# A first modulation by halves of the features, and inverse roots as one power operation on GpSimd

## The chip, the core and the metric

The kernel runs on one core of one Trainium2 chip. The core has five engines: TensorE (PE; its weight loads are listed apart as PEld), VectorE (DVE), ScalarE (ACT), GpSimd (POOL) and SyncE (SP), which here issues most DMAs. Each engine works off its own queue of instructions in order; semaphores tie the queues together. The metric is the device time of one execution in microseconds, the median of several.

## What is computed

Two layers of a backbone over 640 tokens: 512 latent tokens and a prompt of 128, with 1024 features each. The prompt has conditioning of its own, so that scale and shift come in two variants, one for the latent tokens and one for the prompt. Cut to what matters here:

```python
def trunk_layer(x, cond, grid, ctx, ...):
    sh1, sc1, gt1, sh2, sc2, gt2 = modulation(cond, w_mod, b_mod)   # silu(cond) @ w_mod + b_mod
    h = rms_norm(x, g_norm_mix) * (1.0 + sc1) + sh1
    rq, rk, rv, rg, qn, qr, ckv, kr = project(h, w_in, ...)         # h @ w_in; qa, kva, kr normed per row
    ...                                                             # retention, latent attention
    x = x + gt1 * (jnp.concatenate([ret, attn], axis=-1) @ w_o)
    h = rms_norm(x, g_norm_ffn) * (1.0 + sc2) + sh2
    gate, up = jnp.split(h @ w_ffn_in, 2, axis=-1)
    x = x + gt2 * ((jax.nn.silu(gate) * up) @ w_ffn_out)

def rms_norm(x, g):
    y = x * lax.rsqrt(jnp.mean(x * x, axis=-1, keepdims=True) + EPS)
    return y * g
```

Inverse square roots stand in three places: the norms over 1024 features (one root per token), the norms of the low-rank parts qa, kva and kr (three roots per token), and the norms of keys and queries per head.

## The kernel before

The 640 tokens are five tiles of 128, the fifth the prompt; tokens lie on partitions for norms, and features lie on partitions for the operands of a projection. The 1024 features are eight k steps of 128. A float32 product is made of three products of rounded parts: each operand is split into a high part, a rounded copy, and a low part, the rest, and `mm3` (L373 to L375) multiplies high by high, high by low and low by high. So every operand costs a copy (ACT as a rule) and a subtraction (DVE).

A planner puts each engine's instructions in order by the order of the program and by when their operands are ready. `tc.keep_in_program_order` (called `pin`) ties an instruction behind the one that the program put before it on the same engine. Buffers come from pools: 20 large ones of 128 x 1280 (`big`: X0, the operand T, and `wm`, the pieces of modulation weights, share them), 20 of 128 x 512 (`slot`), 12 for weights of 128 x 1024 (`wgt`), and small ones. `prefetch(n)` issues loads of the next weights on SP's queue and splits them into high and low parts (L356, L357) until weights of cost n are ready; `take` hands them out.

The **front** of the first layer (L653 to L668) runs so. `first_norm` (L577) takes for each tile two sums of squares on ACT, one inverse root, the scaling of x (L534), the transposes on PE (L537), and copies into X0, features on partitions. `first_half(i, dst)` (L245) loads 1024 of the modulation's columns, eight pieces of 512 KB on SP's queue, multiplies them by the conditioning on PE (L261, 16 products), adds the bias on DVE (`rows`, L265) and transposes the result into `modT`. It is called for all scale columns first, then for all shift columns. Behind the scales come `gain` (G1 = gain of the norm times one plus scale) and `first_scale` (L584), which multiplies X0 by G1, half on DVE, half on ACT. Then come `prefetch(6)` and `load_consts`, and behind the shifts `first_shift` (L595), which makes the high part on ACT (L603) and the low part in one fused DVE operation, tokens in the groups of `FIRST_MOD`: the first tile, two tiles, two tiles. Then `weave` mixes the projection `low_first` (`low_steps`, L684: eight k steps of 416 columns a tile into `low`, squares on ACT, three roots a token, `lown` at L695 and L696, transposes at L718, `ck` and `qa` behind them), the next modulations (`gemv_steps`, L219, of which `gemv1` loads into the large buffers that X0 and the halves leave), and others.

The **inverse roots**: `rsqrt_of` (L377) does a guess by bits and three Newton steps on DVE, eight operations for one column (L381 to L387) and eleven for three. `rsqrt_act` (L395) takes a logarithm and an exponential on ACT and one Newton step of three operations on DVE. `rsqrt_of` is called 20 times for one column: by `inv_rms` (L522) in `first_norm`, in `norm_quarters` (L557) at the entry of the FFN in both layers, and in `norm_steps` at the start of the second layer, where the roots of all five tiles come first; and ten times for three columns in `low_steps`. `rsqrt_act` is called twice in each of four `pair_steps` (L1013) a layer, for 12 columns of keys and 20 of queries; its result scales the keys, and the queries at L1075 and L1077, and `head_steps` transposes the queries on PE (L1098).

At the **layer boundary** the last projection of the first layer ends in `apply_gate` (`x`, L1230); POOL's queue issues the stores of x to DRAM (L1414); the norms of the second layer follow (`norm_mod`: x at L534, transposes at L537, `htmp`, and the high and low parts, L555). At the entry of the FFN `norm_quarters` writes quarters, and `operand` makes the high and low parts Mh and Ml (L1268).

## Time and profile before

| | |
|---|---|
| median of 3 runs | 1709.63 us (1708.22 to 1710.19) |
| the profiled execution | 1709.34 us |
| its span, first to last instruction | 1707.6 us |
| mean granted clock of TensorE | 0.989 |
| PE, DVE, ACT, POOL busy | 97%, 70%, 43%, 3% |

A row of the profile gives an engine, a line of the kernel, the operation, what it writes and reads by the program's names, the shape and a count. The span runs from the first to the last instruction; the execution's own time is 1.7 us longer. The granted clock is 1.00 where TensorE runs at 2.4 GHz and 0.50 at 1.2 GHz; a value between is a mean over a stretch with both.

### The profile page before, as it was taken

To read this page: it belongs to the slowest core of one execution; us is meant where nothing else is said; L and a number is where in the kernel's file an instruction comes from. 1 tells how busy PE (TensorE), PEld (TensorE's weight loads), DVE (VectorE), ACT (ScalarE), POOL (GpSimd) and SP (SyncE) were. 2 spreads that over 40 slices of the span, in tenths; PEclk is the share of its full clock that TensorE was granted. 3 is DMA by queue.
4 is the path that set the end of the run, shared out by engine and by line. 5 is a ranking of instruction groups with operands and counts; after the bars stand their busy time and mean duration, and the time that the engine had idled before them with its cause. 6 is when DMAs were issued, how large, how long until landed. Compare 5 with 4: busy or idle time off the path is not lost.

```text
span 1707.6 us, 26357 instructions
## 1 busy us (share of the span) xinstructions
PE 1651.3 (97%) x10166; PEld 1422.2 (83%) x10166; DVE 1194.9 (70%) x2670; ACT 741.2 (43%) x1598; POOL 56.4 (3%) x74
## 2 busy tenths in 40 slices
PE   6999999999999999999979999999999999999998
PEld 2789887667988898989959888776789899999987
DVE  5846569737966687776786455787388777686766
ACT  4532258734524242524344222687355243343422
POOL 0001210000000000000010021100000000000000
PEclk9999999999999999999989999999999999999999
DMA  9862101141226322313383420011312231212222
GB/s 325 306 224 70 35 17 32 38 133 65 74 76 218 134 91 76 106 50 112 113 321 105 144 64 26 19 29 62 125 63 90 71 112 62 99 50 99 75 74 87
DMA packets 65407, 173.77 MB, mean 102 GB/s; under 512 B 10353, under 2 KB 19953, under 8 KB 65281
## 3 DMA queue, kind: packets, MB, share of 16 engines
q1 hardware_dynamic: 64288, 169.20, 29.3%
q0 software_dynamic: 800, 2.62, 0.4%
q8 instruction: 80, 1.31, 0.3%
q14 instruction: 47, 0.38, 0.1%
q10 hardware_dynamic: 192, 0.26, 0.1%
HBM read 166.09 MB, written 5.96 MB: 101 GB/s over the span
## 4 chain that ended last, share of the span: by engine, by line
PE 85%; DVE 7%; ACT 4%; DMA 3%; issue 1%; SPq 0%; DVEq 0%; ACTq 0%
PE AB L373 7%; PE AB L375 7%; PE AB L374 7%; PE fo L373 6%; PE fo L375 6%; PE fo L374 6%; PE win L373 3%; PE win L375 3%; PE win L374 3%; PE D L373 3%; PE D L375 3%; PE D L374 3%; PE po L1161 3%; PE gemv L219 2%; PE wo L373 2%; PE wo L374 2%
## 5 line engine op out<-in xcount | busy, mean ns | idle before, releaser
L373 PE MATMUL AB<-Mh,wprod 128*128 128x320 f32 x800 | 248.1, 310 | 0.0
L374 PE MATMUL AB<-Ml,wprod 128*128 128x320 f32 x800 | 247.0, 309 | 0.0
L375 PE MATMUL AB<-Mh,wprod 128*128 128x320 f32 x800 | 245.5, 309 | 0.0
L357 DVE TENSOR_TENSOR wl<-raw,wh 128x1024 fp32r<-128x1024 f32 (+3 forms) x124 | 138.6, 1118 | 119.5 <-ACT wh L356 104.7
L334 ACT CAST wprod<-raw 128x512 fp32r<-128x512 f32 x200 | 121.8, 621 | 230.7 <-PE fo L374 146.0
L356 ACT CAST wh<-raw 128x1024 fp32r<-128x1024 f32 (+3 forms) x124 | 119.5, 964 | 128.3 <-PE wo L374 45.6
L373 PE MATMUL fo<-wh,act 128*128 128x512 f32 x440 | 171.8, 394 | 0.0
L374 PE MATMUL fo<-wl,act 128*128 128x512 f32 x440 | 171.7, 390 | 0.0
L375 PE MATMUL fo<-wh,act 128*128 128x512 f32 x440 | 171.5, 390 | 0.0
L373 PEld LDWEIGHTS AB<-Mh,wprod 128*128 128x128 f32 x800 | 150.2, 188 | 6.3 <-issue 2.5
L374 PEld LDWEIGHTS AB<-Ml,wprod 128*128 128x128 f32 x800 | 150.2, 188 | 0.9
L375 PEld LDWEIGHTS AB<-Mh,wprod 128*128 128x128 f32 x800 | 149.8, 188 | 0.0
L335 DVE TENSOR_TENSOR wprod<-raw,wprod 128x512 fp32r<-128x512 f32 x200 | 134.0, 686 | 22.3 <-ACT wprod L334 22.2
L1229 DVE TENSOR_TENSOR yt<-fo,gt 128x512 f32<-128x512 f32 x120 | 79.0, 686 | 56.5 <-PE fo L375 56.5
L373 PE MATMUL win<-wh,Th 128*128 128x384 f32 x320 | 111.3, 349 | 0.1
L374 PE MATMUL win<-wl,Th 128*128 128x384 f32 x320 | 107.8, 337 | 0.0
L375 PE MATMUL win<-wh,Tl 128*128 128x384 f32 x320 | 107.7, 337 | 0.0
L373 PEld LDWEIGHTS fo<-wh,act 128*128 128x128 f32 x440 | 82.6, 188 | 21.9 <-DVE yt L1229 5.9
L373 PE MATMUL D<-Mh,wprod 128*128 128x320 f32 x320 | 99.2, 310 | 0.0
L375 PE MATMUL D<-Mh,wprod 128*128 128x320 f32 x320 | 99.0, 309 | 0.0
L374 PE MATMUL D<-Ml,wprod 128*128 128x320 f32 x320 | 98.9, 309 | 0.0
L375 PEld LDWEIGHTS fo<-wh,act 128*128 128x128 f32 x440 | 82.6, 188 | 17.7 <-DVE act L914 0.3
(322 smaller groups left out, 3738.6 us busy)
## 6 DMA issues: line engine op xcount, KB each, us to landing
raw<-in_wts_dram SPq DMA_DIRECT2D x140, 512.0 KB
wm<-in_w_mod_dram SPq DMA_DIRECT2D x96, 512.0 KB
raw<-in_wts_dram SPq DMA_DIRECT2D x32, 384.0 KB
raw<-in_wts_dram SPq DMA_DIRECT2D x32, 256.0 KB
x<-in_x_sample_dram SPq DMA_DIRECT2D x16, 256.0 KB
gt<-gt_d SPq DMA_DIRECT2D x16, 256.0 KB
raw<-in_wts_dram SPq DMA_DIRECT2D x8, 416.0 KB
raw<-in_wts_dram SPq DMA_DIRECT2D x8, 320.0 KB
```

Source lines behind the costliest of these rows:

```text
L219: PE.matmul(acc[32 * j:32 * j + 32, :], lhsT=scv[:, k].rearrange("p a b -> p (a b)"), rhs=raws[k, j // 2][:, 512 * (j % 2):512 * (j % 2) + ...
L334: S.copy(out=hi, in_=src)
L335: V.tensor_tensor(out=lo, in0=src, in1=f(hi), op=ALU.subtract)
L356: S.copy(out=hi, in_=raw)
L357: V.tensor_tensor(out=lo, in0=raw, in1=f(hi), op=ALU.subtract)
L373: PE.matmul(ps, lhsT=ah, rhs=bh, start=first, stop=False, skip_group_check=more)
L374: PE.matmul(ps, lhsT=ah, rhs=bl, start=False, stop=False, skip_group_check=more)
L375: PE.matmul(ps, lhsT=al, rhs=bh, start=False, stop=last, skip_group_check=more)
L1161: PE.matmul(o[64 * a:64 * a + 64, :], lhsT=value(p, kt, a), rhs=PTs[2 * p + a][kt], start=(kt == 0), stop=(kt == 4), tile_position=(0, 64 ...
L1229: V.tensor_tensor(out=tmp, in0=ps, in1=gtb["g"][2 * s + h][:, c], op=ALU.mult)
```

## The change

The first modulation is divided by features and no longer by scale and shift. `first_half(i)` loads, for all 1024 rows, the shift and the scale columns of 512 features (i = 0: the first, i = 1: the second), in pieces of 2 KB where they had 4 KB, and yields after every third k step. Of the second half the products of the shift columns (j = 0) are pinned on PE. Each half computes its part of G1 itself. `first_scale` and `first_shift` become `first_mod`, for one half of the features and one group of tokens: DVE scales and shifts in one operation, ACT copies the high part, DVE subtracts; all of DVE's operations are pinned. Between the halves stands `prefetch(4)`. Behind the first half's modulation `low_half` does the first four k steps of the low projection for all five tiles, a part of the second half's products behind each tile; then come the rest of the second half, `prefetch(4)`, `load_consts`, and the second `first_mod`. `low_steps` does the last four k steps on the accumulators already begun (the fifth tile's is in a double bank).

`rsqrt_of` becomes one operation on GpSimd, the element-wise power with an exponent of -0.5 from a constant tile `mhalf`, for any number of columns; `rsqrt_act` is gone, and the pairs call `rsqrt_of`.

```diff
--- before.py
+++ after.py
@@ -188,6 +188,8 @@
     V.memset(ones, 1.0)
     eps_t = cp.tile([P, 1], F32, name="eps_t")
     V.memset(eps_t, EPS)
+    mhalf = cp.tile([P, 32], F32, name="mhalf")
+    V.memset(mhalf, -0.5)
 
 
     modT = [cp.tile([P, 48, 2], F32, name=f"modT{l}") for l in range(NL)]
@@ -242,32 +244,40 @@
                     nc.sync.dma_start(out=gt_d[l][gi][s:s + 1, 512 * j:512 * j + 512], in_=rows[r:r + 1, :])
         yield 0.5
 
-    def first_half(i, dst):
+    def first_half(i):
 
         both = ps2("gemv")
         acc, tr = both[:64, :512], both[:, 512:768]
         raws = []
         for k in range(KD):
-            raw = big([P, 1024], "wm")
-            nc.sync.dma_start(out=raw, in_=w_mod[0, k * P:(k + 1) * P, i * 1024:i * 1024 + 1024])
+            raw = big([P, 2, 512], "wm")
+            nc.sync.dma_start(out=raw, in_=w_mod[0, k * P:(k + 1) * P, 0:2048].rearrange(
+                "p (j h c) -> p j h c", j=2, h=2)[:, :, i])
             raws.append(raw)
         bm = slot([P, 512], "bm")
         for j in range(2):
             nc.scalar.dma_start(out=bm[32 * j:32 * j + 32, :],
-                                in_=b_mod_flat[0, 0, 2 * i + j].unsqueeze(0).broadcast_to([32, 512]))
+                                in_=b_mod_flat[0, 0, 2 * j + i].unsqueeze(0).broadcast_to([32, 512]))
         yield
         for k in range(KD):
             for j in range(2):
-                PE.matmul(acc[32 * j:32 * j + 32, :], lhsT=scv[:, k].rearrange("p a b -> p (a b)"),
-                          rhs=raws[k][:, 512 * j:512 * j + 512], start=(k == 0), stop=(k == KD - 1),
-                          tile_position=(0, 32 * j))
+                m = PE.matmul(acc[32 * j:32 * j + 32, :], lhsT=scv[:, k].rearrange("p a b -> p (a b)"),
+                              rhs=raws[k][:, j], start=(k == 0), stop=(k == KD - 1), tile_position=(0, 32 * j))
+                if i == 1 and j == 0:
+                    tc.keep_in_program_order(m)
+            if k % 3 == 2:
+                yield
         rows = slot([P, 512], "rows")
         V.tensor_tensor(out=rows[:64], in0=acc, in1=bm[:64], op=ALU.add)
         for c in range(4):
             PE.transpose(tr[:, c * 64:(c + 1) * 64], rows[:64, c * P:(c + 1) * P], ident[:64, :64])
         src = tr.rearrange("p (c j s r) -> p j c s r", c=4, j=2, s=2, r=16)
-        V.tensor_copy(out=dst.rearrange("p (j c) s -> p j c s", j=2), in_=src[:, :, :, :, 0])
-        yield
+        dst = modT[0][:, 0:16, :].rearrange("p (j h c) s -> p j h c s", j=2, h=2)[:, :, i]
+        V.tensor_copy(out=dst, in_=src[:, :, :, :, 0])
+        k = slice(4 * i, 4 * i + 4)
+        V.scalar_tensor_tensor(out=G1[:, k], in0=modT[0][:, 8 + 4 * i:12 + 4 * i, :], scalar=1.0,
+                               in1=gc_t[:, 0, C_MIX + 4 * i:C_MIX + 4 * i + 4].unsqueeze(2).broadcast_to([P, 4, 2]),
+                               op0=ALU.add, op1=ALU.mult)
 
     def run(gen):
         for _ in gen:
@@ -377,30 +387,7 @@
     def rsqrt_of(v, w):
 
         y = small(w, "ry")
-        a = small(w, "ra")
-        V.tensor_scalar(out=y.bitcast(I32), in0=v.bitcast(I32), scalar1=-0.5, scalar2=1597463007.0,
-                        op0=ALU.mult, op1=ALU.add)
-        if w == 1:
-            V.tensor_scalar(out=v, in0=v, scalar1=-0.5, scalar2=None, op0=ALU.mult)
-            for _ in range(3):
-                V.tensor_scalar(out=a, in0=y, scalar1=y, scalar2=v, op0=ALU.mult, op1=ALU.mult)
-                V.scalar_tensor_tensor(out=y, in0=a, scalar=1.5, in1=y, op0=ALU.add, op1=ALU.mult)
-            return y
-        for _ in range(3):
-            V.scalar_tensor_tensor(out=a, in0=y, scalar=-0.5, in1=y, op0=ALU.mult, op1=ALU.mult)
-            V.tensor_tensor(out=a, in0=a, in1=v, op=ALU.mult)
-            V.scalar_tensor_tensor(out=y, in0=a, scalar=1.5, in1=y, op0=ALU.add, op1=ALU.mult)
-        return y
-
-    def rsqrt_act(v, w):
-
-        y = small(w, "ry")
-        a = small(w, "ra")
-        S.activation(out=y, in_=v, func=AF.Ln)
-        S.activation(out=y, in_=y, func=AF.Exp, scale=-0.5)
-        V.scalar_tensor_tensor(out=a, in0=y, scalar=-0.5, in1=y, op0=ALU.mult, op1=ALU.mult)
-        V.tensor_tensor(out=a, in0=a, in1=v, op=ALU.mult)
-        V.scalar_tensor_tensor(out=y, in0=a, scalar=1.5, in1=y, op0=ALU.add, op1=ALU.mult)
+        GP.tensor_tensor(out=y, in0=v, in1=mhalf[:, :w], op=ALU.pow)
         return y
 
     ORDER = (0, 1, 2, 3, 4)
@@ -581,27 +568,24 @@
                 S.copy(out=X[2 * h][:, :, tok(t)], in_=ps[:, 0:2])
                 V.tensor_copy(out=X[2 * h + 1][:, :, tok(t)], in_=ps[:, 2:4])
 
-    def first_scale(X, G):
-        for j in range(4):
+    def first_mod(X, G, SH, T, half, cols):
+
+        pin = tc.keep_in_program_order
+        lo_of = None
+        for j in (2 * half, 2 * half + 1):
             for kk in range(2):
                 k = 2 * j + kk
-                for a, b, s in ((0, 512, 0), (512, 640, 1)):
+                for a, b, s in cols:
                     x = X[j][:, kk, a:b]
-                    if kk == 0:
-                        V.tensor_scalar(out=x, in0=x, scalar1=G[:, k, s:s + 1], scalar2=None, op0=ALU.mult)
-                    else:
-                        S.activation(out=x, in_=x, func=AF.Copy, scale=G[:, k, s:s + 1])
-
-    def first_shift(X, SH, T):
-        for g in FIRST_MOD:
-            for j in range(4):
-                for kk in range(2):
-                    k = 2 * j + kk
-                    for a, b, s in g:
-                        x, sh = X[j][:, kk, a:b], SH[:, k, s:s + 1]
-                        hi, lo = T[0][j][:, kk, a:b], T[1][j][:, kk, a:b]
-                        S.activation(out=hi, in_=x, func=AF.Identity, bias=sh)
-                        V.scalar_tensor_tensor(out=lo, in0=x, scalar=sh, in1=f(hi), op0=ALU.add, op1=ALU.subtract)
+                    pin(V.tensor_scalar(out=x, in0=x, scalar1=G[:, k, s:s + 1], scalar2=SH[:, k, s:s + 1],
+                                        op0=ALU.mult, op1=ALU.add))
+            c = slice(cols[0][0], cols[-1][1])
+            S.copy(out=T[0][j][:, :, c], in_=X[j][:, :, c])
+            if lo_of is not None:
+                pin(lo_of())
+            lo_of = lambda j=j, c=c: V.tensor_tensor(out=T[1][j][:, :, c], in0=X[j][:, :, c], in1=f(T[0][j][:, :, c]),
+                                                     op=ALU.subtract)
+        pin(lo_of())
 
     def gain(l, g_col, sc_chunk, name):
         G = lp.tile([P, KD, 2], F32, tag=name, name=nm(name))
@@ -653,19 +637,15 @@
         if l == 0:
             X0 = [big([P, 2, TT], "X0") for _ in range(4)]
             T = new_T()
+            G1 = lp.tile([P, KD, 2], F32, tag="G1", name=nm("G1"))
             first_norm(xs_next, X0)
-            scale, shift = first_half(1, mT[:, 8:16]), first_half(0, mT[:, 0:8])
-            next(scale)
-            next(shift)
-            next(scale)
-            G1 = gain(l, C_MIX, 8, "G1")
-            first_scale(X0, G1)
-            next(shift)
-            prefetch(6)
-            load_consts()
-            first_shift(X0, mT, T)
-            done.update((l, "T", t) for t in ORDER)
-            X0 = None
+            halves = [first_half(0), first_half(1)]
+            next(halves[0])
+            prefetch(4)
+            next(halves[1])
+            run(halves[0])
+            for g in FIRST_MOD:
+                first_mod(X0, G1, mT, T, 0, g)
         else:
             G1 = gain(l, C_MIX, 8, "G1")
             T = new_T()
@@ -673,18 +653,28 @@
         ck = big([P, 2, TT], "ck", F32R)
         KR = lp.tile([P, 6, 32], F32, tag="KR", name=nm("KR"))
 
-        def in_tok_mm(ws, t, w, ps):
-            assert (l, "T", t) in done
-            n = KD // len(ws)
-            for k in range(KD):
+        def in_tok_mm(ws, t, w, ps, ks=range(KD)):
+            assert (l, "T", t) in done or ks.stop < KD
+            n = KD // 4
+            for k in ks:
                 wh, wl = ws[k // n]
                 c = slice((k % n) * w, (k % n + 1) * w)
                 mm3(ps, Tk(T, k, tok(t)), (wh[:, c], wl[:, c]), k == 0, k == KD - 1)
 
+        low_ps = {}
+
+        def low_half(ws, t):
+
+            low_ps[t] = ps1("low") if t < 4 else ps2("low")
+            in_tok_mm(ws, t, 416, low_ps[t][:, :416], range(KD // 2))
+
         def low_steps(ws, t):
-            ps = ps1("low")
+            if t in low_ps:
+                ps, ks = low_ps.pop(t), range(KD // 2, KD)
+            else:
+                ps, ks = ps1("low"), range(KD)
             pa, pk = ps[:, :256], ps[:, 256:416]
-            in_tok_mm(ws, t, 416, ps[:, :416])
+            in_tok_mm(ws, t, 416, ps[:, :416], ks)
             xn = slot([P, 416], "lown")
             v = small(3, "v")
             S.activation(out=xn[:, :256], in_=pa, func=AF.Square, scale=1.0 / 16.0, accum_out=v[:, 0:1])
@@ -763,7 +753,7 @@
                 yield
 
         def low_first():
-            low_w.extend(take(4, "in_low"))
+            low_w.extend(take(4 - len(low_w), "in_low"))
             for t in ORDER:
                 lows[t] = low_steps(low_w, t)
                 next(lows[t])
@@ -775,6 +765,17 @@
                 yield
 
         if l == 0:
+            low_w.extend(take(2, "in_low"))
+            for t in ORDER:
+                low_half(low_w, t)
+                next(halves[1], None)
+            run(halves[1])
+            prefetch(4)
+            load_consts()
+            for g in FIRST_MOD:
+                first_mod(X0, G1, mT, T, 1, g)
+            done.update((l, "T", t) for t in ORDER)
+            X0 = None
             log_gammas()
         if l == 0:
             gemv1 = gemv_steps(l, 1, ahead=AHEAD)
@@ -1037,7 +1038,7 @@
             v = small(32, "kv")
             V.tensor_reduce(out=v[:, 0:12], in_=jk, axis=AX.X, op=ALU.add)
             V.tensor_scalar(out=v[:, 0:12], in0=v[:, 0:12], scalar1=EPS, scalar2=None, op0=ALU.add)
-            r = rsqrt_act(v[:, 0:12], 12)
+            r = rsqrt_of(v[:, 0:12], 12)
             Kv = KH.rearrange("p t a e -> p (t a) e")
             V.tensor_tensor(out=Kv[:, :, 0:64], in0=Kv[:, :, 0:64],
                             in1=r.unsqueeze(2).broadcast_to([P, 12, 64]), op=ALU.mult)
@@ -1059,7 +1060,7 @@
             V.tensor_reduce(out=v[:, 22:32], in_=jq[:, :, 64:96], axis=AX.X, op=ALU.add)
             V.tensor_scalar(out=v[:, 12:22], in0=v[:, 12:22], scalar1=EPS, scalar2=None, op0=ALU.add)
             V.tensor_scalar(out=v[:, 22:32], in0=v[:, 22:32], scalar1=2.0, scalar2=EPS, op0=ALU.mult, op1=ALU.add)
-            r = rsqrt_act(v[:, 12:32], 20)
+            r = rsqrt_of(v[:, 12:32], 20)
             Qr = Qv[:, :, 64:96]
             V.tensor_tensor(out=Qr[:, 8:10], in0=Qr[:, 8:10], in1=gqr[:, l].unsqueeze(1).broadcast_to([P, 2, 32]),
                             op=ALU.mult)
```

## Rows read from the trace of the kernel before

**Rows 1.** The page: busy us, share of the span and instructions of each engine.

```profile
PE 1651.3 (97%) x10166; PEld 1422.2 (83%) x10166; DVE 1194.9 (70%) x2670; ACT 741.2 (43%) x1598; POOL 56.4 (3%) x74
```

**Rows 2.** By stretches: length, busy us by engine, PEclk, DMA share, GB/s.

```profile
core 0: us, PE busy (x) PEld busy (x) DVE busy (x) ACT busy (x) POOL busy (x), PEclk, DMA share, GB/s
6.00:10.00 4.00, 0.11 (x1) 0.11 (x2) 2.41 (x11) 2.17 (x6) 0.00 (x0) 1.00 0.97 344
28.90:40.20 11.30, 8.67 (x39) 2.38 (x38) 5.84 (x15) 5.82 (x12) 0.00 (x0) 1.00 1.03 398
442.00:448.00 6.00, 4.47 (x22) 3.71 (x21) 5.91 (x9) 4.05 (x7) 0.00 (x0) 0.82 0.64 201
870.00:893.00 23.00, 13.71 (x74) 8.40 (x73) 21.68 (x82) 13.40 (x39) 2.70 (x5) 0.70 0.91 332
```

**Rows 3.** Groups by line and shape: busy us, mean ns, idle before, its releasers.

```profile
L373 PEld LDWEIGHTS low<-wh,Th 128*128 128x128 f32 x80 | 15.3, 192 | 4.1 <-DVE ck L723 1.2 <-ACT Th L603 1.1 <-PE lowT L718 0.8
```

**Rows 4.** Timeline of the front: start us, us, instruction, idle before and releaser.

```profile
25.25 3.88 PE L261 MATMUL gemv<-wm,scv 128*32 128x512 f32 x16
...
28.91 0.68 DVE L265 TENSOR_TENSOR rows<-gemv,bm 64x512 f32<-64x512 f32 x1 [2.72 <-PE gemv L261]
...
38.32 0.68 DVE L265 TENSOR_TENSOR rows<-gemv,bm 64x512 f32<-64x512 f32 x1 [2.14 <-PE gemv L261]
...
40.22 0.46 PE L373 MATMUL low<-wh,Th 128*128 128x416 f32 x1 [0.70 <-ACT Th L603]
...
52.90 1.04 PE L219 MATMUL gemv<-wm,scv 128*32 128x512 f32 x2
...
53.88 0.46 PE L374 MATMUL low<-wl,Th 128*128 128x416 f32 x1
```

**Rows 5.** Waits from 40 to 140 us: engine, releaser, total us, times, longest.

```profile
PEld lowT L718 <- DVE lown L695: 1.3, 1, 1.3
...
PEld low L373 <- DVE ck L723: 1.2, 1, 1.2
```

**Rows 6.** Groups by line and shape: two operations of the inverse roots.

```profile
L386 DVE TENSOR_SCALAR ra<-ry,v 128x1 f32<-128x1 f32 x60 | 16.3, 271 | 1.7
...
L391 DVE TENSOR_TENSOR ra<-ra,v 128x3 f32<-128x3 f32 x30 | 4.8, 160 | 0.8
```

**Rows 7.** Timeline of the layer boundary.

```profile
875.94 1.14 POOL L1414 DMA_DIRECT2D x_d<-x  x2 [1.26 <-DVE x L1230]
...
877.37 0.14 DVE L381 TENSOR_SCALAR ry<-v 128x1 int32<-128x1 int32 x1
...
879.25 0.49 DVE L534 TENSOR_SCALAR x<-x,ry 128x512 f32<-128x512 f32 x1
...
879.79 1.97 PE L537 MATMUL nT<-ident,x 128*128 128x128 f32 x8 [4.04 <-DVE x L534]
...
887.88 0.48 DVE L534 TENSOR_SCALAR x<-x,ry 128x512 f32<-128x512 f32 x1
...
890.93 0.69 PE L373 MATMUL low<-wh,Th 128*128 128x416 f32 x1
```

**Rows 8.** Instructions of one line: shortest/median/longest ns, first and last start, shapes.

```profile
L939 POOL TENSOR_TENSOR vd<-qkv,KDt x32: 394/613/1317, 131.7 to 1069.5; 128x256 f32<-128x256 f32 x16, 128x128 f32<-128x128 f32 x16
...
L884 DVE TENSOR_TENSOR qkv<-rt x32: 411/414/780, 124.5 to 1068.6; 128x256 f32<-128x256 f32 x32
```

**Rows 9.** Timeline of the entry of the first layer's FFN.

```profile
445.72 0.59 PE L374 MATMUL gu<-Ml,wh 128*128 128x320 f32 x1 [1.25 <-DVE Ml L1268]
```

**Rows 10.** Timeline of the first two attention pairs of the first layer.

```profile
238.31 0.17 DVE L1061 TENSOR_SCALAR kv<-kv 128x10 f32<-128x10 f32 x1
...
239.67 0.82 DVE L1075 TENSOR_TENSOR QH<-QH,ry 128x640 f32<-128x640 f32 x1
...
241.00 0.13 PEld L1098 LDWEIGHTS qT<-ident,QH 128*96 128x96 f32 x1 [0.24 <-DVE QH L1077]
...
268.33 0.48 DVE L1077 TENSOR_TENSOR QH<-QH,ry 128x320 f32<-128x320 f32 x1
...
269.78 0.60 PE L1098 MATMUL qT<-ident,QH 128*96 128x128 f32 x4
```

## Prediction

> **What bounds the kernel now.** I read the page first: TensorE (PE) is busy 97% of the 1707.6 us span, DVE 70%, ACT 43%, POOL 3% [rows 1]. An edit that frees DVE or ACT is therefore worth only what it takes from the stretches in which PE waits. I looked for those in the table by stretches [rows 2] and read each in the order of time. Three touch the change. In the front, PE's busy time from 28.9 to 40.2 us is 8.67 of 11.3 us, with the DMA engines full (share 1.03). At the layer boundary PE is busy 13.71 of 23 us from 870 to 893, DVE 21.68, and the granted clock averages 0.70 there. At the entry of the FFN (442 to 448) PE has 4.47 of 6 us, DVE 5.91, clock 0.82. At the last two PE waits for DVE; in the front PE, DMA and a short chain share the time.
>
> The profiled execution took 1709.34 us, its span 1707.6; it lies 0.3 us under the median of 1709.63. I take the sum from 1709.34.
>
> **Part one, the first modulation by halves.** Before, all scale columns come first, then all shift columns; the low projections wait for both. After, the first 512 features get scale and shift, and half of each tile's k steps (60 of 120 products) can run before the second 512 features are done.
>
> Each low product needs a weight load of 192 ns [rows 3], and they follow each other at that pace, so 60 of them are 11.5 us. The tempting sum is that they vanish behind the second half's transfers. The rows speak against it: PE is not free there. A modulation half has 32 records; 16 of them take 3.88 us [rows 4], so it is some 7.8 us of PE, and the second half's must run somewhere in the same stretch. What can be won is only PE's idle time. So I lay out PE from the end of the first half's product (DVE's `rows` at 28.91) to the point where 60 low products are done [rows 4]:
> - Before: the second `rows` starts at 38.32, low at 40.22, about 0.4 us lost at its first lo operand, then 11.5 us: 52.1.
> - After: from `rows` to the first product took 1.9 us before (38.32 to 40.22); the scale is now in that chain and the lo is pinned behind the next two scalings, I add 1.0. Start 31.8. Then 11.5 of low, 7.8 of modulation, 0.5 of transposes. PE changes three times between the two kinds: the two records at 52.90 hold it until 53.88, 0.98 us against 0.5 at the pace above, so about 0.5 us lost per excursion, 1.5 to 2 us for three. Sum 53.4.
>
> So the reordering itself loses about 1.3 us. Against that stand two gains. The first norms no longer occupy DVE with inverse roots, so the transposes are out of the first products' way (up to 1 us; the transfers then bound that half). And at 40 to 140 us PE and its weight loads wait 1.3 us for DVE's `lown` and 1.2 us for `ck` [rows 5]; DVE has less to do there, I count 1.3 us of that. Net gain 1 us, range from 4 lost to 4 won.
>
> The modulation's DVE and ACT work changes little: DVE did scalings and fused subtractions before and does fused scale-shifts and subtractions after; it runs beside PE's 21 us. Transfers: the pieces become 2 KB. The nearest row with 2 KB pieces is the loading of x in the stretch from 6 to 10 us, 344 GB/s at a share of 0.97 [rows 2] against 398 at 1.03, about 8% per busy share; 4.2 MB of a half take 10.5 us at 398, so 0 to 0.9 us, 0.5 taken, covered in the second half because PE reaches its last two k steps only at about 45 us. Three `in_low` pieces (1.3 MB, 3.2 us) now stand on SP's queue ahead of the second half; the second half would land near 41 us, still covered by the same. If PE got there earlier, these 3 us would show. The constants stay behind the halves and are needed later. The fourth `in_low` piece comes behind the second half, and DVE's second modulation is pinned behind its splitting; it lands about 1 us after the half, long before DVE needs to go on.
>
> **Part two, inverse roots on POOL.** Removed from DVE: 20 calls of one column (three of L386 each, [rows 6]) of 8 operations, 10 calls of three columns (three of L391 each) of 11, and 3 of the 5 operations of the 16 calls in the pairs; ACT loses 2 in each of these. A one-column call takes DVE 1.88 us when nothing stands between (877.37 to 879.25, [rows 7]) and some 1.6 us packed. In all about 56 us of DVE, most of it off the path.
>
> What a power operation costs on POOL the trace doesn't show. The nearest rows are POOL's multiplications: 394 ns at the least, 613 median and 1317 at the most for 128 or 256 columns [rows 8]. For one to three columns I bound it by 0.4 and 1.3 us and take 0.6 (a power is more work per column, but there is one). For 12 or 20 columns the ends are 0.4 and 4 us (three of the longest one); I take 1.5.
>
> *Layer boundary* [rows 7]. DVE's chain: first root at 877.37, x of tile 0 at 879.25, x of tile 2 at 887.88, first low product at 890.93. PE's order has the transposes of tiles 0, 1 and 2 ahead of that product. Four calls (tiles 0 to 3) lie on a full DVE before 890, 4 x 1.6 = 6.4 us. POOL's own queue has the stores of x first (last issues 875.94 to 877.08), so the first power starts near 877.4, no later than DVE's did. What is late next is the rest of DVE's work (x, htmp, Tl) and PE's eight transposes a tile at the lower of the clock's levels (1.2 GHz), 1.97 us at 879.79; I give back 1 us for that and 1 us for POOL's round trips: 4.5 us won, 2 to 6.5.
>
> *FFN entry* [rows 9], in each layer. PE waits 1.25 us at 445.72 for DVE's Ml, in the stretch in which DVE is busy 5.91 of 6 us; a call of 1.6 us lies in DVE's full queue ahead of it. I take the whole wait, 1.25 us a layer, 2.5 us; ends 0 and 4 (1.6 and a shorter stay at the lower clock).
>
> *Attention pairs* [rows 10]. The chain from the sums of Q (238.31) through ACT, DVE, L1075 (239.67) to PE's load at 241.00, which waits for L1077, has no slack in the first pair. It spends about 1.2 us between the sum and L1075. 1.5 us and two hand-overs make it some 0.5 us longer. Freed DVE and ACT time gives a little back; POOL takes some (below). I take 1 us lost in all, 5 lost to 2 won.
>
> **POOL and DVE together.** The rows show that the two get in each other's way: `qkv<-rt` on DVE takes 414 ns median and 780 at the most, `vd` on POOL 613 and 1317 [rows 8], though `qkv<-rt` has one shape throughout. The Trainium skill, SBUF — State Buffer, section "SBUF: two separate sides", says that the pair of ports that DVE and GpSimd share is locked for a whole instruction and that the loser waits. By that rule every power could hold DVE up for its whole length; the two maxima agree with it in kind. As a mechanism of this kernel it is rival B.
>
> **Sum.** 1 + 4.5 + 2.5 - 1 = 7 us: 1709.3 - 7 = 1702.3, forecast 1702.5.
>
> **Rivals.**
> - A, the front loses. The next modulation (`gemv1`) loads into buffers that X0 and the second half hold; half of X0 is now held until the second features are modulated, by the layout above behind the 60th product, where before all of X0 was free ahead of it. If PE's order keeps `gemv1` where it was, its k steps wait for 2 to 4 us of transfers, and part one gives -4 instead of +1: 1707.3. For it: DMA share was 1.03 in this stretch. Against: two X0 tiles come free earlier than before.
> - B, POOL blocks DVE: the 16 powers of the pairs, 24 us of POOL, hold DVE up where it stands on the chain; attention loses 5 us rather than 1, the boundary wins 3: 1707.8. Against: of the 32 `qkv<-rt` the median (414 ns) is the minimum (411), so most are not held [rows 8].
> - C, slower: a power of 20 columns takes about 8 us, where the rows have 0.4 to 1.3 for any POOL operation. Place: the Q chain of the pairs. It grows by 6.8 us; the first pair has no slack, the second 1 us (L1077 ends at 268.8, the transpose starts at 269.78, [rows 10]), the others I count at 1 us together: 6.8 + 5.8 + 1 per layer, 27 us in two layers. With the other gains at 8: 1709.3 + 27 - 8 = 1728. It decides from about 4 us for 20 columns. Against it: POOL's shortest operation on 128 columns takes 394 ns [rows 8], and one column at 3.6 us or less (887.88 less 877.1, by three) still gains at the boundary.
> - D, more: PE's shorter idle time keeps its clock at the higher level (2.4 GHz) at the boundary, where the transposes then cost half, and DVE's stalls behind the front vanish whole: 6.5 at the boundary, 4 in the front, 4 at the FFN, 1 lost in the pairs: 1695.8.
> - That the change doesn't do what it says: the planner may still place second-half modulation products ahead of the low ones; only half of them are pinned to program order. The front then stays as before, 1703.3, within the forecast.
>
> **How the numbers follow.** About 0.2% (3.4 us) is what a measurement of this kernel can tell from no change, so faster means under 1706.2. Forecast 0.52 (1697 to 1707), A 0.15, B 0.10, C 0.12, D 0.11. Faster: 0.49 + 0.11 + 0.06 from A and B = 0.66. Slower: C and a little of A = 0.14. Same: 0.20. The range reaches from D's time less 2 us to A and B with their spread, 1693 to 1712, and leaves C and a little of D out.
>
> **What would show it.** POOL gets 46 new operations: one column near 0.6 us, 20 columns near 1.5; over 4 us means C. First low product near 31.8 us and the 60th near 53; PE's idle time from 28.9 to 52 not smaller than before. At the boundary the first low product 9 to 10 us after the last FFN product's gate instead of 15, DVE no longer full. PE's wait for Ml at the FFN entry under half of its 1.25 us. I am wrong if the first stage moves by more than 4 us either way or the pairs stretch by over 3 us a layer.

## The result, and the profile after

| | before | after |
|---|---|---|
| median | 1708.93 us (4 runs beside it) | 1732.51 us (4 runs, 1730.33 to 1736.23) |
| ratio | | 1.0146, interval 1.0118 to 1.0174 |
| span of the profiled execution | 1707.6 us | 1731.8 us |

The changed kernel is 25 us slower (20 to 30). The forecast was 1702.5 us with a range up to 1712. Rival C, a power too slow for the attention pairs, named the place and the sign; it priced 1728.

The page's first view answers [rows 1]. DVE and ACT are freed as planned, POOL has 46 operations more and takes over twice the time; PE's busy time rises although it does the same 10166 products.

```profile
PE 1662.4 (96%) x10166; PEld 1429.0 (83%) x10166; DVE 1153.4 (67%) x2368; ACT 728.5 (42%) x1538; POOL 124.8 (7%) x120
```

Where the 24 us of span came from is seen if each trace is cut at the first products of the stages. Lengths in us, from the start times of those products, here also for four of the runs told of below (E1 to E4):

| stretch | before | after | E1 | E2 | E3 | E4 |
|---|---|---|---|---|---|---|
| start to the first wide projection | 113.7 | 115.1 | 115.7 | 115.3 | 119.2 | 115.1 |
| attention pairs, layer 1 (first `kvb` to first `wo`) | 146.1 | 163.4 | 143.8 | 143.8 | 143.8 | 164.9 |
| first `wo` to first `AB`, layer 1 | 83.5 | 82.6 | 82.6 | 83.5 | 82.7 | 83.5 |
| first `AB` to first `fo`, layer 1 | 39.5 | 37.7 | 37.7 | 38.0 | 37.7 | 38.0 |
| layer boundary (last `fo` to first `low`) | 20.0 | 16.1 | 16.1 | 20.0 | 16.1 | 20.0 |
| attention pairs, layer 2 | 142.9 | 156.0 | 142.9 | 142.9 | 142.8 | 161.8 |
| first `wo` to first `AB`, layer 2 | 83.4 | 82.6 | 82.6 | 83.5 | 82.6 | 83.4 |

The two attention stages take 17.3 and 13.1 us more. All the rest together is 6 us less. By stretches, the kernel before, the two attention stages and the boundary (columns as in [rows 2]):

```profile
211.10:357.20 146.10, 137.65 (x944) 105.66 (x942) 111.02 (x281) 100.62 (x267) 8.96 (x11) 0.98 0.14 40
1057.40:1200.30 142.90, 134.20 (x945) 105.10 (x943) 110.66 (x270) 100.34 (x267) 8.93 (x11) 0.98 0.14 41
...
870.90:890.90 20.00, 10.71 (x64) 5.64 (x63) 18.99 (x72) 12.13 (x35) 2.69 (x5) 0.71 0.90 324
```

The same of the changed kernel, and one stretch of its front:

```profile
31.00:36.00 5.00, 5.00 (x16) 3.55 (x16) 5.00 (x14) 1.83 (x3) 0.00 (x0) 0.50 1.05 384
...
213.20:376.60 163.40, 147.48 (x944) 112.92 (x942) 109.83 (x257) 98.36 (x251) 32.31 (x19) 0.92 0.12 36
1071.20:1227.20 156.00, 138.55 (x944) 108.56 (x943) 109.22 (x246) 97.74 (x251) 32.31 (x19) 0.96 0.12 37
...
889.50:905.60 16.10, 10.25 (x65) 5.54 (x63) 13.89 (x35) 10.29 (x30) 5.79 (x10) 0.79 0.85 296
```

In the pairs DVE has less to do and yet the stage is longer. PE does the same products; its busy time grows by 9.8 and 4.4 us, beside a mean granted clock that falls from 0.98 to 0.92 and 0.96, and its idle time by 7.5 and 8.7 us. What the powers cost, by shape, and DVE's waits for them (changed kernel):

```profile
L390 POOL TENSOR_TENSOR ry<-kv,mhalf 128x20 f32<-128x20 f32 x8 | 28.2, 3531 | 56.6 <-DVE kv L1062 56.6
L390 POOL TENSOR_TENSOR ry<-kv,mhalf 128x12 f32<-128x12 f32 x8 | 19.2, 2398 | 99.6 <-DVE kv L1040 99.6
L390 POOL TENSOR_TENSOR ry<-v,mhalf 128x1 f32<-128x1 f32 x20 | 12.0, 598 | 242.7 <-DVE v L514 242.7
L390 POOL TENSOR_TENSOR ry<-v,mhalf 128x3 f32<-128x3 f32 x10 | 8.8, 882 | 80.2 <-DVE v L683 80.2
```

```profile
DVE QH L1076 <- POOL ry L390: 26.1, 8, 3.6
DVE KH L1043 <- POOL ry L390: 12.3, 8, 2.2
DVE lown L685 <- POOL ry L390: 7.8, 10, 1.0
```

A power takes 0.60 us for one column, 0.88 for three, 2.40 for 12 and 3.53 for 20: each column more adds about 0.15 us ((3.53 - 0.60) / 19). The first pair, in order of time, answers [rows 10]:

```profile
241.18 0.17 DVE L1062 TENSOR_SCALAR kv<-kv 128x10 f32<-128x10 f32 x1
241.43 3.53 POOL L390 TENSOR_TENSOR ry<-kv,mhalf 128x20 f32<-128x20 f32 x1 [4.05 <-DVE kv L1062]
...
244.99 1.10 DVE L1076 TENSOR_TENSOR QH<-QH,ry 128x640 f32<-128x640 f32 x1 [3.64 <-POOL ry L390]
...
246.41 0.68 DVE L1095 TENSOR_TENSOR kT<-kT,kT 96x512 fp32r<-96x512 f32 x1
...
246.55 0.65 PE L1099 MATMUL qT<-ident,QH 128*96 128x128 f32 x4 [1.90 <-DVE QH L1078]
```

From the last sum to the scaling of the queries it is 3.81 us (241.18 to 244.99), where it was 1.36 (238.31 to 239.67 in [rows 10]): 2.45 us more. DVE's queue stands meanwhile, and PE waits for the queries.

### The profile page after: what moved, and what is told of

Read it like the earlier page. It is cut to its first block, busy times and chain, and to the rows that moved or that the text cites. A ratio compares the mean times of both kernels' runs of the same rounds, so it can differ in the third digit from the quotient of the medians.

```text
span 1731.8 us, 26106 instructions
## 1 busy us (share of the span) xinstructions
PE 1662.4 (96%) x10166; PEld 1429.0 (83%) x10166; DVE 1153.4 (67%) x2368; ACT 728.5 (42%) x1538; POOL 124.8 (7%) x120
## 4 chain that ended last, share of the span: by engine, by line
PE 80%; DVE 8%; POOL 3%; DMA 3%; issue 3%; ACT 3%; SPq 0%; DVEq 0%; ACTq 0%; POOLq 0%
PE AB L383 7%; PE AB L384 6%; PE AB L385 6%; PE fo L383 6%; PE fo L385 6%; PE fo L384 6%; PE win L383 3%; PE win L385 3%; POOL ry L390 3%; PE win L384 3%; PE D L383 3%; PE D L385 3%; PE D L384 3%; PE gemv L221 2%; PE wo L383 2%
## 5 line engine op out<-in xcount | busy, mean ns | idle before, releaser
L367 DVE TENSOR_TENSOR wl<-raw,wh 128x1024 fp32r<-128x1024 f32 (+3 forms) x124 | 138.4, 1117 | 130.0 <-ACT wh L366 115.7
L344 ACT CAST wprod<-raw 128x512 fp32r<-128x512 f32 x200 | 121.7, 621 | 231.9 <-PE fo L384 146.1
L383 PEld LDWEIGHTS fo<-wh,act 128*128 128x128 f32 x440 | 82.6, 188 | 23.3 <-DVE yt L1230 7.4
L385 PEld LDWEIGHTS fo<-wh,act 128*128 128x128 f32 x440 | 82.6, 188 | 17.7 <-DVE act L915 0.3
```

The costliest lines, as they stand in the source:

```text
L344: S.copy(out=hi, in_=src)
L367: V.tensor_tensor(out=lo, in0=raw, in1=f(hi), op=ALU.subtract)
L383: PE.matmul(ps, lhsT=ah, rhs=bh, start=first, stop=False, skip_group_check=more)
L385: PE.matmul(ps, lhsT=al, rhs=bh, start=False, stop=last, skip_group_check=more)
```

## The experiments

Theory P: the powers of 12 and 20 columns in the pairs are the whole loss. Theory O: the other edits brought another order of work, and the pairs only show it. The first four runs take the change apart.

**E1, the pairs as before.** `rsqrt_act` is put back, and only the pairs call it.

```diff
-            r = rsqrt_of(v[:, 0:12], 12)
+            r = rsqrt_act(v[:, 0:12], 12)
...
-            r = rsqrt_of(v[:, 12:32], 20)
+            r = rsqrt_act(v[:, 12:32], 20)
```

> The changed kernel with one thing undone: the keys' and queries' roots of the attention pairs are made on ACT and DVE again; the front by halves and the powers of one and three columns stay. Theory P (the loss is the powers of 12 and 20 columns in the pairs, 2.3 and 3.5 us each, for which DVE stands still 38 us in all): the two attention stages give back the 30.5 us by which they grew, and the kernel lands 5 to 8 us under the kernel before, near 1702. Theory O (the loss comes from another order of the work in the attention, set off by the front and the norms, and the powers only show where the time is): under half of it comes back, and the kernel stays above 1715.

Measured: 1700.97 us, ratio to before 0.9954 (0.9941 to 0.9966), 7.9 us faster. All of the attention's loss is gone (table above). Theory P holds, O falls. (In E1, E2 and E3 the first attention stage has the order of the kernel before and takes 143.8 us where it took 146.1: so much one execution differs from another there.)

**E2, the front by halves alone**: the changed kernel with all roots of the kernel before.

> The front by halves alone, all roots as before. By the two traces the changed kernel starts its first wide projection 1.4 us later and its first pair 2.1 us later than the kernel before. Theory F1 (the halves lose a little by themselves, TensorE falls to the lower clock in them): 1 to 3 us slower than before, 1710 to 1712. Theory F2 (the reordering is even, what was lost in the front came from the powers of three columns there): within 1 us of before. Theory F3 (the powers freed DVE in the front and hid a larger loss): 4 us or more slower.

Measured: 1709.18 us, ratio 1.0006 (0.9994 to 1.0017): 1 us slower, between 1 us faster and 3 slower. F1 and F2 are not told apart; F3 falls.

**E3, the powers of one and three columns alone**, in the kernel before:

```diff
     def rsqrt_of(v, w):
         y = small(w, "ry")
...
+        GP.tensor_tensor(out=y, in0=v, in1=mhalf[:, :w], op=ALU.pow)
         return y
```

> The kernel before with the power on GpSimd for the roots of one and three columns only; front and pairs as before. By the traces of before and after the stages from the output projection to the second layer's first projection took 5.3 us less, the second layer's last part 2.8 us less, the rest 0.3: theory P expects 7 to 9 us faster than before, 1700 to 1702. A rival (those gains came from the pairs' lateness, a second layer that starts later with more loaded ahead) expects under 3 us.

Measured: 1704.01 us, ratio 0.9972 (0.9961 to 0.9982), 4.8 us faster. It falls between the two expectations. By the table the boundary gives 3.9 us and the FFN entries about 1 us each, as in E1, but the front is 5.5 us longer than before. Part of that is PE's only wait there from 60 to 120 us, behind a root of three columns:

```profile
PE low L375 <- DVE lown L688: 1.8, 1, 1.8
```

Another is the second half's product: PE's loads waited 8.7 us for its transfers in this execution (5.1 before), and the granted clock is 0.76 from 33 to 47 us. The front by halves has no such wait in E1; so the two parts together give 7.9 us, 4 more than the sum of E2 and E3 (1.0 lost, 4.8 won). Each of the three intervals reaches some 2 us to either side, so the size of these 4 is open.

**E4, the powers of 12 and 20 columns alone**, in the kernel before: `rsqrt_pow` in the two calls of E1's diff.

> The kernel before with the power on GpSimd for the keys' and queries' roots of the pairs only. Theory P: 28 to 33 us slower than before, 1737 to 1742, the two attention stages 17 and 13 us longer. Theory O (the pairs are slow only in the order that the other edits bring about): under 15 us slower.

Measured: 1737.70 us, ratio 1.0175 (1.0155 to 1.0196), 29.9 us slower. Theory P holds also from this side. (Its profiled execution was its slowest, 1745.62 us; the table's attention stages are long by that.)

Now what it is about the powers. Theory W: DVE stands and waits. Theory S: POOL at work holds DVE up. Theory C: only the length of the chain to PE's transposes counts.

**E5, powers beside the chain**: the kernel before, and each `rsqrt_act` of the pairs issues a power that nobody reads.

```diff
+        GP.tensor_tensor(out=scr[:, :w], in0=v, in1=mhalf[:, :w], op=ALU.pow)
         S.activation(out=y, in_=v, func=AF.Ln)
```

> The kernel before, with the 16 powers of the pairs added beside the old roots: GpSimd takes each power into a scratch tile that nobody reads, and the chain goes over ACT and DVE as before. Theory W (DVE waits for the result and its queue stands): GpSimd's 47 us of powers cost next to nothing, within 3 us of the kernel before. Theory S (GpSimd at work holds DVE up through what the two share): a good part of the 29 us that the powers in the pairs cost shows here too, 8 us or more slower.

Measured: 1712.84 us, ratio 1.0028 (1.0017 to 1.0038): 4.6 us slower (3 to 6.5), of 29.9. Between the two; S is a sixth of the loss, a fifth at the most. And not even that is DVE being held up. In the shade of a whole power the two scalings of the queries (L1091 and L1093 here) take 0.82 and 0.48 us, as in [rows 10]:

```profile
238.28 3.54 POOL L411 TENSOR_TENSOR scr<-kv,mhalf 128x20 f32<-128x20 f32 x1 [3.40 <-DVE kv L1077]
...
239.31 0.82 DVE L1091 TENSOR_TENSOR QH<-QH,ry 128x640 f32<-128x640 f32 x1
240.05 0.48 DVE L1093 TENSOR_TENSOR QH<-QH,ry 128x320 f32<-128x320 f32 x1
```

What the powers do hold up is POOL's own queue: `vdp`, a multiplication, comes behind them, and PE waits for it, which it did not before. This is a part of the 4.6 us; the rest is not placed.

```profile
PEld UP L1017 <- POOL vdp L907: 1.4, 2, 0.7
PE UP L1017 <- POOL vdp L907: 0.9, 2, 0.5
```

**E6, the keys' powers covered.** E4, with the scaling of keys and queries one step later in the order and pinned on DVE. The cut below shows the keys; the queries' scaling gets a step (`yield 0.1`) and pins likewise, and the planner's lists of steps get one more entry a pair for it.

```diff
...
             r = rsqrt_pow(v[:, 0:12], 12)
+            yield 0.7
             Kv = KH.rearrange("p t a e -> p (t a) e")
-            V.tensor_tensor(out=Kv[:, :, 0:64], in0=Kv[:, :, 0:64],
-                            in1=r.unsqueeze(2).broadcast_to([P, 12, 64]), op=ALU.mult)
+            pin(V.tensor_tensor(out=Kv[:, :, 0:64], in0=Kv[:, :, 0:64],
+                                in1=r.unsqueeze(2).broadcast_to([P, 12, 64]), op=ALU.mult))
...
```

> The kernel with the powers in the pairs only (29 us slower than before), where the scaling of the keys and queries is put one step later and pinned on DVE: 11, 16, 6 and 3 operations now stand in DVE's order between a key power's input and its use, where 1 to 3 stood; for the queries one as before. The powers stay as long as they are. Theory W: DVE's 12 us of waiting for the keys' powers shrink to under 5 and the time by 5 to 12 us, to 17 to 24 us over before. Theory C (it is the length of the chain from the projection over the power to TensorE's transposes that counts, whatever DVE does meanwhile): within 4 us of the powers in the pairs, 25 us or more over before.

Measured: 1730.21 us, ratio 1.0134 (1.0112 to 1.0156), 22.9 us slower than before (19 to 26.5), 7 better than E4. Its six executions lie in two groups of three, near 1726.5 and near 1735, and the profiled one (1734.51) is of the second. DVE's waits (E6):

```profile
DVE QH L1087 <- POOL ry L411: 20.2, 8, 3.5
DVE kv L1047 <- ACT jk L1042: 9.6, 6, 3.1
DVE qt L1081 <- ACT QH L1062: 3.1, 2, 1.5
DVE KH L1052 <- POOL ry L411: 0.9, 2, 0.5
```

The keys' wait fell from 12.3 to 0.9 and the queries' from 26.1 to 20.2; DVE's waits for ACT rose from 3.0 us in the kernel before to 12.7. By its time it is inside what W expects and outside what C expects, but not by much: the interval reaches C's 25.

**E7, the power for the queries alone.**

> The kernel before with the power on GpSimd for the queries' roots alone (20 columns, 3.53 us each); the keys' stay on ACT and DVE. DVE waited 26.1 us for the queries and 12.3 for the keys. Theory W (time follows DVE's standing): about two thirds of the 29 us, 17 to 22 us slower than before. Theory Q, the reading of the prediction (only the queries' chain has no slack): nearly all, 26 us or more. A third (the keys, which come first in each pair, delay everything behind them): under 14.

Measured: 1733.04 us, ratio 1.0153 (1.0132 to 1.0174), 26.1 us slower (22.6 to 29.7). This is theory Q's side: the queries' powers are 26 of the 30 us, though in the changed kernel a third of DVE's standing is for the keys. The 12.3 us for the keys cost about 4, which the intervals of E4 and E7 don't tell from nothing. W in its simple form, time in proportion to DVE's standing, expected 17 to 22 and just falls outside.

**E8, idle products in the front's stop.** E1, with eight products into an accumulator that is overwritten, ahead of the first low product.

```diff
...
             low_w.extend(take(2, "in_low"))
+            low_ps[0] = ps1("low")
+            for _ in range(8):
+                tc.keep_in_program_order(PE.matmul(low_ps[0][:, :P], lhsT=ident, rhs=ident, start=True, stop=True))
...
```

> The front by halves and the powers of one and three columns, pairs as before (7.8 us faster than before), with eight idle products of 128 x 128 put on TensorE between the first half's transposes and the first low product, where it stands still for 1.9 to 2.4 us and the granted clock then reads 0.50 for 6 us. Their result is overwritten. Theory K (this stop is what lets the clock fall, and the products at half speed make the halves lose what they win): the clock stays at 1.00 from 30 to 37 us, the first wide projection starts 2 to 3 us earlier, the time falls by 2 to 3 us. Theory D (in this stretch the transfers of the second half set the pace): the clock stays up, the first low products take half the time, but the start of the first wide projection moves by under 1 us.

Measured: 1699.77 us, ratio 0.9957 (0.9942 to 0.9972); E1 had 0.9954. The clock stays up and the same five microseconds hold 23 records, where the changed kernel had 16 at 0.50:

```profile
31.00:36.00 5.00, 4.74 (x23) 2.71 (x24) 4.91 (x12) 2.62 (x5) 0.00 (x0) 1.00 1.05 383
```

From the first low product to the first wide projection it is 82.8 us against 84.5 in E1, 1.7 less; in the medians no gain is seen. Theory K is right on the clock and too high on the gain.

**E9, keys and queries covered**, by E6's edit with the step of the queries' scaling placed later still.

> As the run with the keys covered, and now the scaling of the queries too stands later in DVE's order: 5, 8, 3 and 6 operations lie between the power's input and its use, where 0 or 1 did. The powers stay as long as they are, 3.53 us for 20 columns. Theory W (what costs is that DVE's queue stands until the power is there): DVE's 20 us of waiting for the queries shrink to under 8 us and the time to 5 to 12 us over before. Theory C (what costs is the length of the chain to TensorE's transposes, which the later place makes longer): 20 us or more over before, as with the keys covered (22 us).

**E10, the same order with the old roots**, the control for E9.

> The same order as the run with keys and queries covered, with the old roots on ACT and DVE: what the later place of the two scalings costs or gives by itself. Within 3 us of the kernel before if the place is free. If it costs 5 us or more, that much of the run with the powers covered is the order's and not the powers'.

Measured: E9 1730.64 us, ratio 1.0137 (1.0121 to 1.0153), 23 us slower than before; E10 1728.93 us, 1.0129 (1.0113 to 1.0144), 22 us slower. In E9 DVE waits only 4.2 us for the queries' powers and 0.9 for the keys', and yet the time is E6's. Taken alone this would speak for C. But E10 has the same edit without the powers and is as slow, so, by its own condition, the 22 us of E9 are the order's and not the powers'. What E10 does show is that late queries are enough: with the old roots, an order in which the keys and queries are scaled later costs nearly as much as the slow powers did. PE's waits for the queries in E10:

```profile
PE qT L1110 <- DVE QH L1089: 13.1, 2, 6.5
PE qT L1110 <- DVE sum L1147: 2.9, 2, 1.5
```

Between E9 and E10 the powers cost 1.7 us, which the intervals don't tell from nothing. Both theories expect that: DVE hardly stands for the powers any more (W), and the chain is hardly longer by them (C). So these two runs don't decide between W and C. POOL's work as such is not what costs 26 us (E5); late queries can cost as much by themselves (E10); what part DVE's standing has in it is open.

One rival is left, that the powers act by way of the planner. It orders each engine's instructions by when their operands are ready, so a longer root also changes the order. If the records of the second attention stage are put beside those of the kernel before, E1, E2 and E5 have the same order on PE, DVE and ACT; in E7 about 30 of PE's 942 products and 30 of DVE's 246 operations (the roots left out) stand elsewhere, in E4 and the changed kernel somewhat more, in E10 over 100 of each. No run has the slow powers on the chain in the old order, so how much of the 26 us is the longer chain and how much the other order is not shown.

**E11, one block.** E8, with the second half's products in one block behind the third tile and not in four between the tiles.

```diff
                 low_half(low_w, t)
-                next(halves[1], None)
+                if t == 2:
+                    run(halves[1])
```

> As the run with the eight idle products (8.5 us faster than before), and the second half's 16 pairs of products stand in one block behind the third tile's low products, where they stood in four blocks between the tiles. TensorE then changes between the two kinds of products once and not four times. The prediction priced such a change at 0.5 us: theory E expects the first wide projection 1.5 us earlier, 1 to 2 us faster than with four blocks. Theory D (the second modulation comes later by the block, and TensorE waits for it): 0 to 2 us slower.

Measured: 1701.17 us, ratio 0.9963 (0.9950 to 0.9976), against 0.9957 in E8. No gain; in the trace the first wide projection starts at 114.1 us in both.

**E12, three columns on DVE.** E1, with the old `rsqrt_of` for the low-rank norms.

> The front by halves with the powers of one column only; the roots of three columns (0.85 us each on GpSimd, for which DVE waited 7.8 us in ten places) are on DVE again, pairs as before. Theory W: DVE's waiting for the three columns was off TensorE's way, within 1.5 us of the same kernel with those powers (7.8 us faster than before). Its rival (each such wait delays the transposes behind it): 2 to 4 us faster than that kernel.

Measured: 1698.08 us, ratio 0.9946 (0.9932 to 0.9959), 9.2 us faster than before and 1.3 faster than E1, within the intervals: theory W's side, as far as this can tell.

**E13, the first stop of the pairs filled.** What stayed open is the lower clock in the pairs. E4, with eight idle products ahead of the first queries' transposes of each layer.

> The kernel with the powers in the pairs only (29 us slower than before), with eight idle products of 128 x 96 put on TensorE in the first pair of each layer, after var and ahead of the queries' transposes, where it stands still for 2.5 us; the granted clock reads 0.50 for the next 7.5 us. Their result is overwritten, the powers and the waits stay. Theory K (a part of the loss is the lower clock behind each stop): the clock stays at 1.00 from 246 to 253 us and each layer's attention is 2 to 4 us shorter, 4 to 8 us in all. Theory C alone (only the longer chain counts; DVE and ACT set the pace behind the stop): the clock stays up and the time stays within 2 us of the powers in the pairs.

Measured: 1745.97 us, ratio 1.0223 (1.0209 to 1.0237), 8 us slower than E4: neither. The stretch behind the stop, first in E4, then in E13:

```profile
244.00:252.00 8.00, 6.16 (x31) 5.02 (x31) 6.92 (x12) 3.76 (x8) 0.71 (x2) 0.60 0.00 0
```

```profile
244.00:252.00 8.00, 6.84 (x63) 5.72 (x63) 5.87 (x11) 3.82 (x10) 0.00 (x0) 1.00 0.00 0
...
PE UP L1009 <- POOL vdp L899: 4.6, 1, 4.6
```

The clock stays up, and from the first queries' transposes to the second it is 6.6 us (244.24 to 250.83) against 8.6 in E4 (245.84 to 254.44): with the clock up this stretch is 2 us shorter. But then PE comes early to the next wait, 4.6 us for `vdp`, which stands behind the keys' power in POOL's queue. The planner has also put ACT's, DVE's and PE's work in another order here, so the total tells nothing on the clock. Its share of the loss stays open.

**E14, combined**: E12 with E8's idle products.

> What the runs so far point to: the front by halves with the eight idle products, the powers of one column only, the roots of three columns on DVE, pairs as before. If the two small gains add up (three columns on DVE 1.4 us, idle products 0.7 to 1.6 us), 1696 to 1698, 11 to 12 us faster than the kernel before; if they cover the same wait, as the run with three columns on DVE, 1698.

Measured: 1699.45 us, ratio 0.9949 (0.9936 to 0.9963). The two small gains don't add up. E12 is the best version seen: 34 us faster than the changed kernel, 9 faster than the one before.

## Why the prediction was wrong

**The step that failed is the pairs.** The sum took 1 us lost, with ends of 5 lost and 2 won. It is 30 us (E4). The prediction's own sign of being wrong, pairs longer by over 3 us a layer, came with 17.3 and 13.1. Two terms of it failed, the price and the slack.

- The price. A power of 12 or 20 columns was bounded by 0.4 and 4 us, and 1.5 taken. It is 2.40 and 3.53, inside the bounds, near the upper end. The value was chosen from POOL's multiplications [rows 8], as if one instruction had one price; a power grows by 0.15 us with each column.
- The slack. The prediction gave the first pair of a layer none, the second 1 us, the others nearly full cover, from one gap of 1 us between two rows [rows 10]. By the measured chain (2.45 us longer) that reading would have cost 2.45 + 1.45 and little more a layer, some 8 us in all. E7 has 26 for the same eight calls (21 in its profiled execution, one of its two faster ones). Where they arise is seen in the queries' transposes of the first layer, those of the first head of a pair and, for the second pair, of both heads, with the clock behind the second pair's; first before, then in E7:

```profile
241.43 0.60 PE L1098 MATMUL qT<-ident,QH 128*96 128x128 f32 x4
...
268.80 0.41 PE L373 MATMUL S<-kT,qh 96*128 96x320 f32 x1
...
271.94 0.64 PE L1098 MATMUL qT<-ident,QH 128*96 128x128 f32 x4
...
296.72 0.64 PE L1098 MATMUL qT<-ident,QH 128*96 128x128 f32 x4
...
268.80:273.00 4.20, 4.12 (x31) 3.84 (x32) 4.19 (x11) 3.49 (x10) 0.00 (x0) 1.00 0.01 4
```

```profile
245.81 0.78 PE L1106 MATMUL qT<-ident,QH 128*96 128x128 f32 x4 [2.10 <-DVE QH L1085]
...
275.40 0.61 PE L1106 MATMUL qT<-ident,QH 128*96 128x128 f32 x4 [2.45 <-DVE sum L1143]
...
277.55 0.47 PE L375 MATMUL S<-kT,qh 96*128 96x320 f32 x1
...
281.60 1.05 PE L1106 MATMUL qT<-ident,QH 128*96 128x128 f32 x4
...
308.30 0.64 PE L1106 MATMUL qT<-ident,QH 128*96 128x128 f32 x4
...
277.00:283.00 6.00, 5.83 (x25) 5.70 (x26) 4.55 (x12) 4.52 (x14) 0.00 (x0) 0.50 0.01 3
```

The stage starts at 211.07 us before and at 213.15 in E7. Counted from there, the queries of the first pair are 2.3 us late, those of the second 3.5 (269.78 in [rows 10]): up to here the prediction's slack holds (2.45, then 1.45 more). Then it breaks: the second head of the second pair is 7.6 late, the third pair 9.5, the fourth 11.5, and the stage ends 10.0 later (10.8 in the second layer). So the two pairs that were taken as covered, and what stands between the heads of the second, cost the most, which no term of the sum held. At that place PE has stood for 2.45 us and soon after for 0.8 more, the granted clock reads 0.50 from 277 to 283 us, where the kernel before has 1.00 at the same work, and six products `S` (from 277.55) stand behind the second pair's first transposes that stood ahead of them before (from 268.80). How the 4 us gained there divide among the stop, the clock and the order is not shown.
- So rival C was the right mechanism in its place and sign, with the wrong threshold: it was to decide from 4 us and cost 27 us at 8. The pairs cost 30 at 3.5. Even with the slack read as none in any pair and the upper bound of the price, 4 us in place of the old 1.2, the pairs would have come to some 22 us lost and the sum to about 1724, short of the 1732.5 measured; a range that took in this bound would have had the sign right.

**Rival B falls as a mechanism.** It priced 4 us more in the pairs, and the powers beside the chain do cost 4.6 (E5), but not by holding DVE. The rows of POOL and DVE in each other's way were multiplications [rows 8], and there the changed kernel agrees: beside `vdp` the scaling of the keys takes 1.79 us, without it 0.96.

```profile
237.42 0.96 DVE L1043 TENSOR_TENSOR KH<-KH,ry 128x768 f32<-128x768 f32 x1 [2.15 <-POOL ry L390]
...
263.38 1.79 DVE L1043 TENSOR_TENSOR KH<-KH,ry 128x768 f32<-128x768 f32 x1 [1.36 <-POOL ry L390]
...
264.31 1.75 POOL L892 TENSOR_TENSOR vdp<-pv,KDt 128x512 f32<-128x512 f32 x1
```

Beside a power DVE runs at its own pace (E5). The Trainium skill, SBUF — State Buffer, section "SBUF: two separate sides", has the shared ports held for a whole instruction, and of a DVE operation with two operands in SBUF it says that it takes part in this against a GpSimd operation that reads SBUF. By that the scalings in E5, which have two and lie wholly within a power that reads SBUF, would have had to wait. For powers the measurement decides against it; the multiplications agree in kind.

**The boundary was right**: 4.5 us predicted, 3.9 measured (20.0 to 16.1, in E1 and E3 too), and the first powers start behind the stores as said. Against [rows 7]:

```profile
894.48 1.14 POOL L1415 DMA_DIRECT2D x_d<-x  x2 [1.26 <-DVE x L1231]
895.64 0.78 POOL L390 TENSOR_TENSOR ry<-v,mhalf 128x1 f32<-128x1 f32 x1
896.45 0.88 DVE L521 TENSOR_SCALAR x<-x,ry 128x512 f32<-128x512 f32 x2 [0.46 <-POOL ry L390]
...
905.56 0.46 PE L383 MATMUL low<-wh,Th 128*128 128x416 f32 x1
```

From store to scaled x it is 1.97 us, where it was 3.31 (875.94 to 879.25); DVE's busy time falls from 18.99 of 20.0 to 13.89 of 16.1 us. (The prediction's sum of DVE's freed time took a root of three columns as eleven operations; the code has ten. In all DVE's busy time fell by 41.5 us where the sum had about 56; no term of the forecast was worked out from it.)

**The FFN entry was right in size and wrong in place.** Predicted 1.25 us a layer; the stretch to the first `AB` is 0.8 to 0.9 us shorter, the next 0.3 shorter than in E2 and E4, which have the old roots there. But the wait named for it [rows 9] stands as before:

```profile
464.02 0.42 PE L384 MATMUL gu<-Ml,wh 128*128 128x320 f32 x1 [1.25 <-DVE Ml L1269]
```

**The front stayed inside its range, on the losing side; the layout ended too early and missed the clock.** Predicted 1 us won, between 4 lost and 4 won. By the table the first wide projection starts 1.4 us later (2.0 in E1). The halves alone lose 1 (E2); beside the powers of one and three columns they win 3 (E1 against E3). The layout compared the 60th low product, 53.4 after against 52.1 before. It starts at 52.8 against 54.4, so up to there the change wins. But the next modulation's products, which the layout left out, start at 59.9 where they started at 51.1, and end 1.4 us later. From 28.9 us to the first wide projection PE's idle time falls from 3.4 to 1.7 us and its busy time grows from 81.4 to 84.5: what was won in waits went into products at the lower clock. The first low product was forecast at 31.8 us and came at 30.37. But PE stood still ahead of it, and that was not in the sum:

```profile
27.52 0.46 PE L273 MATMUL gemv<-ident,rows 64*128 64x64 f32 x4 [0.79 <-DVE rows L271]
30.37 0.71 PE L383 MATMUL low<-wh,Th 128*128 128x416 f32 x1 [2.40 <-ACT Th L583]
```

Behind this stop the granted clock is 0.50, the lower level of 1.2 GHz, from 31 to 36 us, where the kernel before kept 1.00; E8 has it at 1.7 us of this stretch. The price of the changes between the two kinds of products did not show: one change and not four gave nothing (E11). Rival A did not come as described: the next modulation's products start later, but wait only 0.7 us for transfers in all (0.4 before).

## What to carry to other kernels

Price a new operation by its columns and not by its name: bound it at the widest place where it is used, and where the bounds straddle the chain's length, take the far end for a chain without slack. A gap between two rows gives the slack of that place and no more: in E7 the first two pairs were as late as their gaps said, and most of the loss came behind them. Lateness is not paid one for one either: in E7 the first pair's queries come 2.3 us late and the stage is 10 longer, in E10 they come 7.3 late and it is 9 longer. And where a planner orders the work, a longer step changes the order too, so a control with the old operations in the new order (E10) belongs to every run that moves something. Take a change apart by where it is used: the same power won 3.9 us at the boundary with one column and lost 26 in the pairs with 20.

## What the runs showed of the hardware

- GpSimd's power costs 0.60 us for one column of 128 partitions, 0.88 for 3, 2.40 for 12 and 3.53 for 20; while it runs, DVE's operations keep their durations (0.82 and 0.48 us), which they don't always beside GpSimd's multiplications (1.79 for 0.96 beside `vdp`).
- A stop of TensorE of 2.4 us was followed by a granted clock of 0.50 for over 5 us in the front, and one of 2.45 us in E7's pairs by 0.50 from 277 to 283 us; idle products in it kept the clock at 1.00 (E8, E13), which in the pairs only brought TensorE earlier to the next wait.
